# A stick-breaking layer rebuilt on sigmoids and a reversed scan, with a respaced HGRN2 layer, in a four-layer decoder trunk

## The chip, the cores and the metric

The kernel runs on one core of a Trainium2 chip as one launch. The metric is the device time of that launch in microseconds (us): 2760.55 before, the median of three runs (2756.59 to 2761.02). The core's engines each work through a queue of their own, in order: TensorE (PE: matmuls and transposes; PEld is its weight load), VectorE (DVE), ScalarE (ACT), GpSimd (POOL) and SyncE (SP, which issues the transfers). They wait for each other by semaphores.

## The reference, cut to what matters

One batch of 512 tokens with 1024 features goes through four layers, each a token mixer and a gated FFN, each with modulation before and a LayerNorm over the residual behind. The change touches the mixers of layer 1 (HGRN2, 8 heads of 128) and layer 3 (stick-breaking attention, 16 heads of 64).

```python
# HGRN2, in chunks of 32 tokens
scores = einsum(q * exp(b - b_ref), k * exp(b_ref - b))        # b: cumsum of log f in the chunk
o_intra = einsum(where(causal, scores, 0), v)
def step(S, (qd, kd, vc, dec)):
    o = einsum('bthd,bhdv->bthv', qd, S)
    S = dec[..., None] * S + einsum('bshd,bshv->bhdv', kd, vc)
...
# stick-breaking, per block of 128 queries t over all keys s before them
z = einsum('bthd,bshd->bhts', q, k)          # q already times 64 ** -0.5
neg_log_1mb = where(valid, softplus(z), 0)   # valid: s < t
later = cumsum(neg_log_1mb, axis=s, reverse=True) - neg_log_1mb
a = where(valid, exp(log_sigmoid(z) - later), 0)
o = einsum('bhts,bshd->bthd', a, v)
```

Since exp(log_sigmoid(z)) is sigmoid(z) and exp(-softplus(z)) is sigmoid(-z), a(t,s) is also sigmoid(z(t,s)) times the product of sigmoid(-z(t,s')) over s < s' < t.

## The kernel before

Activations lie feature-major in SBUF as a high and a low part (fp32r), and every projection takes three matmuls for each product (high by high, low by high, high by low). A *unit* is one 128x1024 block of weights: a transfer into a `raw` buffer (three of them), a cast to the high part on ACT (L255), a subtraction for the low part on DVE (L257), and 24 matmuls of 512 columns. `up` (L285) makes one block of 128 features from a unit; the `down` helpers (L354, L406) make token-major output and hand each piece to `evict`, which adds it to the residual X and at the end of a token block t runs the LayerNorm and the transposes (`tr`) for the next sublayer. `settle` (L480, L481) multiplies and shifts X by the LayerNorm's gain and bias, eight DVE operations that are not needed before the next residual; they take two of the `raw` buffers while they run.

**HGRN2** (`hgrn`). After the values (`p_hv`) come 24 units, q, f and gate for each head (`p_hqf`, `p_hg`). `decay(hd)` makes the decayed queries and keys of a head (QP, KP, QD, KD) on ACT and DVE. `mix(hd)` is a generator in six pieces: `hkz` transposes KD; `hS` makes the scores; `hkv` the 15 chunk products, and behind them on DVE the state chain S (L859), 15 steps, each from the one before; `ho` first the part inside a chunk (L866, *intra*), then 32-row tiles from the states (L870, *inter*, which reads S step by step); `hot` transposes the result. PE's order is written out by hand: units stand at whole numbers, the pieces of a pair's two heads at `d` plus the numbers in HA and HB (HA_END, HB_END for the last pair, whose `d` comes two units earlier), and the list is sorted. The other engines are ordered by the scheduler, by the order of emission and by `high_priority`. `settle` is called when the second pair's decays are emitted. The last pair is filled with the output projection (`down_late`): `early` gives the (half, weight pair) steps that are put among the pieces, `bridge` those that follow, and what is left goes token block by token block at the end.

**Stick-breaking** (`stick`). After the values (`p_sv`) and `settle`, each of 8 pairs of heads takes two units (`p_sqk`, L285), scores z with keys on the partitions (L1236; two fp32r matmuls each, since q and k are stored with their low parts in the other head's rows), a softplus in four passes on ACT and DVE over 1280 columns, its cumulative sum over the keys by matmuls with triangles of ones (L1265, c), exp, a mask, and the product with the values (L1284, so; fp32, two heads side by side). STEPS sets the order of emission; PE's order is the scheduler's.

Of the kernel before, what the change touches and what calls it, by code (L numbers as in the profile page):

```python
# [72 lines left out]
def pack(inp):  # L73
# [70 lines left out]
class Trunk:  # L144
# [243 lines left out]
    def down_late(self, w, nk, act, name, evict, early, bridge, gate=None, rowc=None):  # L388
# [8 lines left out]
        def load(h, kp):  # L397
            return self.unit(w, h * npair + kp, name, None if gate is None else gate[:, h * T:(h + 1) * T], rowc)
# [27 lines left out]
        hls = [[load(h, kp) for kp in left[h]] for h in range(2)]  # L426
# [290 lines left out]
    def hgrn(self, nxt):  # L717
# [4 lines left out]
        with tc.tile_pool(name="hg", bufs=1, reuse_waits="tile") as op, ExitStack() as es:  # L722
# [42 lines left out]
            self.down(ins["hv"], KD, hid, "hv", 2, put_v, head=HEAD)  # L765
            self.psum(mm="01", sc="2", kv="3456", sm="7")
# [59 lines left out]
            def mix(hd, stag, QP, KP, QD, KD_, dec):  # L826
# [30 lines left out]
                for n in range(NC - 1):  # L857
                    Sn = hp.tile([P, P], F32, tag="S", bufs=SB, name=f"S{hd}_{n}")
                    nc.vector.scalar_tensor_tensor(out=Sn, in0=Ss[n], scalar=dec[:, n:n + 1],  # L859
                                                   in1=pv[n % 4][:, n // 4 * P:(n // 4 + 1) * P], op0=ALU.mult, op1=ALU.add)  # L860
                    Ss.append(Sn)
# [65 lines left out]
            next(run[H - 1])  # L927
            self.psum(mm="345601", tr="27")
# [220 lines left out]
    def stick(self, nxt):  # L1149
# [3 lines left out]
        offs = [0, 512, 1024, 896]  # L1153
        with tc.tile_pool(name="so", bufs=1, reuse_waits="tile") as op, ExitStack() as es:
# [11 lines left out]
            stri = kp.tile([P, P], F32, name="stri")  # L1166
            nc.sync.dma_start(out=stri, in_=ins["stri"])
            smask = kp.tile([P, P], I32, name="smask")
            nc.sync.dma_start(out=smask, in_=ins["smask"])
            nu = self.sp.tile([P, T], F32, tag="u", bufs=4, name="nu")[:, 0:P]  # L1170
            nc.sync.dma_start(out=nu, in_=ins["negu"])
            negu = kp.tile([P, P], F32R, name="negu")
            nc.vector.tensor_copy(negu, nu)
            negone = kp.tile([P, P], F32R, name="negone")
            nc.vector.tensor_scalar(out=negone, in0=self.onesr.bitcast(F32), scalar1=-1.0, scalar2=None, op0=ALU.mult)
            self.psum(mm="01", z="237", c="456")
            with tc.issue_after(last[-1].ins):
                nc.scalar.preload_act_table_set("natural_log_exp_and_others")
            gate = self.gate_rows(op, i, 0, "mm")
            free = [(kp, f"n{j}") for j in range(QKS)] + [(op, f"o{j}") for j in range(2 * KD)]  # L1180

            def slot(name, keep=False):
                s = next(f for f in free if not keep or f[0] is op)
                free.remove(s)
                z = s[0].tile([P, T], F32R, tag=s[1], name=name)
                z_slot[name] = s
                return z

            def drop(name):
                s = z_slot.pop(name)  # L1190
                free.insert(sum(f[0] is kp for f in free) if s[0] is kp else len(free), s)

            z_slot = {}
            own = [slice(HD * hh, HD * hh + HD) for hh in range(2)]
            seg = ((0, 512), (512, 1024), (1024, 1280))

            def diags(z):

                return (z[:, 0:1024].rearrange("p (a c) -> p a c", a=2)[:, :, 0:P],
                        z[:, 896:1152].rearrange("p (a c) -> p a c", a=2))  # L1200

            def two(m):
                return m.rearrange("p (a c) -> p a c", a=1).broadcast_to([P, 2, P])

            def queries(p):

                qs = [slot(f"sq{p}{hh}") for hh in range(2)]
                pq = self.up(ins["sqk"], p, "sqk")
                for hh in range(2):
                    r, o = own[hh], own[1 - hh]  # L1210
                    nc.scalar.mul(qs[hh][r, :], pq[r, :], HD ** -0.5)
                    nc.vector.scalar_tensor_tensor(out=qs[hh][o, :], in0=pq[r, :], scalar=HD ** -0.5,
                                                   in1=qs[hh][r, :].bitcast(F32), op0=ALU.mult, op1=ALU.subtract)
                return qs

            def keys(p):
                ks, kx = ([slot(f"{n}{p}{hh}") for hh in range(2)] for n in ("sk", "sx"))
                pk = self.up(ins["sqk"], KD + p, "sqk")
                for hh in range(2):
                    r, o = own[hh], own[1 - hh]  # L1220
                    nc.scalar.copy(ks[hh][r, :], pk[r, :])
                    nc.vector.tensor_tensor(out=ks[hh][o, :], in0=pk[r, :], in1=ks[hh][r, :].bitcast(F32), op=ALU.subtract)
                    nc.scalar.copy(kx[hh][o, :], pk[r, :])
                    nc.vector.tensor_copy(kx[hh][r, :], ks[hh][o, :].bitcast(F32))
                return ks, kx

            def scores(p, hh, qs, ks, kx):
                zt = kp.tile([P, 1280], F32, tag="zt", bufs=ZTB, name=f"zt{p}{hh}")
                for g, (s0, s1) in enumerate(seg):
                    zb = self.bank(f"z{g}_{p}{hh}", "z")  # L1230
                    for sb in range(NT):
                        lo, hi = max(s0, offs[sb]), min(s1, offs[sb] + T - sb * P)
                        if lo < hi:
                            t0 = sb * P + lo - offs[sb]
                            for kk in (ks, kx):
# [164 lines left out]
```

## Time and profile before

| | |
|---|---|
| median of three runs | 2760.55 us |
| the profiled execution, its own time | 2756.47 us |
| its span, first to last instruction | 2754.6 us |
| HGRN2, first q unit to first FFN matmul | 671.5 to 937.6 us |
| stick-breaking, first q unit to first FFN matmul | 2141.4 to 2376.7 us |

The times of rows are microseconds from the span's start. PE's matmuls are pipelined: a matmul of 512 columns is listed with 0.39 us, but the next starts 0.23 us later, so prices are taken from start to start. A tile's name is the program's; a fp32 matmul is two records, a transpose or an fp32r matmul one.

### The profile page before, as it was taken

How to read it: one execution, taken by the hardware profiler on the slowest of the kernel's cores; microseconds unless marked ns; L12 is line 12 of the kernel's file. 1: busy time of each engine (PE TensorE's matmuls, PEld its weight loads, DVE VectorE, ACT ScalarE, POOL GpSimd, SP SyncE). 2: the span in 40 equal slices, each digit the busy share in tenths (PEclk: the TensorE clock that was granted, in tenths of full speed). 3: DMA queues.
4: the chain of work that ended last, by engine and by line, in shares of the span. 5: the costliest groups of instructions: out<-in, count | busy, mean ns of one | idle time of the engine just before them, and what ended most of it. 6: DMA issues, size and time to landing. Idle time of an engine off the chain costs nothing.

```text
span 2754.6 us, 33739 instructions
## 1 busy us (share of the span) xinstructions
PE 2655.6 (96%) x12980; PEld 2128.7 (77%) x12980; DVE 2027.7 (74%) x3133; ACT 1270.9 (46%) x1773; POOL 43.7 (2%) x80
## 2 busy tenths in 40 slices
PE   7979999999998999999999999999999999999998
PEld 5538888877776788887887777888887777888886
DVE  7558997674777699667756777997676688766676
ACT  3134433345674443334545444443334798543432
POOL 0000000000000000000000000000000000000000
PEclk9989999999999999999999999999999999999999
DMA  9844874222221386232222322873333211333222
GB/s 322 235 110 155 299 236 143 95 100 89 85 72 45 126 295 222 92 102 92 98 79 77 97 79 95 276 258 121 100 103 99 62 48 31 106 100 110 97 92 77
DMA packets 109673, 352.33 MB, mean 128 GB/s; under 512 B 12104, under 2 KB 22600, under 8 KB 109512
## 3 DMA queue, kind: packets, MB, share of 16 engines
q1 hardware_dynamic: 109512, 350.17, 38.5%
q8 instruction: 102, 1.67, 0.2%
q14 instruction: 59, 0.48, 0.1%
HBM read 341.63 MB, written 8.50 MB: 127 GB/s over the span
## 4 chain that ended last, share of the span: by engine, by line
PE 79%; DVE 9%; ACT 8%; DMA 2%; issue 2%; POOL 1%; SPq 0%; POOLq 0%; DVEq 0%; ACTq 0%
PE p_f L285 34%; PE p_d L354 16%; PE p_mup L285 5%; PE p_pw L285 3%; PE p_mdn L354 3%; PE p_hqf L285 2%; PE p_hv L354 1%; PE p_sv L354 1%; PE pc L683 1%; PE p_pw L354 1%; PE p_hg L285 1%; PE p_hwo L406 1%; PE ms L977 1%; PE tr L512 1%; ACT hf L517 1%
## 5 line engine op out<-in xcount | busy, mean ns | idle before, releaser
L285 PE MATMUL p_f<-hh,wh_f 128*128 128x512 f32 (+1 forms) x1504 | 565.4, 377 | 1.5 <-ACT hh L523 1.5
L285 PE MATMUL p_f<-hl,wh_f 128*128 128x512 f32 (+1 forms) x1504 | 566.5, 377 | 0.0
L285 PE MATMUL p_f<-hh,wl_f 128*128 128x512 f32 (+1 forms) x1504 | 565.6, 376 | 0.0
L255 ACT CAST wh_f<-r_f 128x1024 fp32r<-128x1024 f32 x176 | 185.2, 1054 | 345.1 <-PE p_f L285 310.1
L285 PEld LDWEIGHTS p_f<-hh,wh_f 128*128 128x128 f32 x1504 | 284.0, 189 | 53.1 <-ACT hh L523 1.8
L285 PEld LDWEIGHTS p_f<-hl,wh_f 128*128 128x128 f32 x1504 | 284.2, 189 | 51.1 <-issue 0.2
L285 PEld LDWEIGHTS p_f<-hh,wl_f 128*128 128x128 f32 x1504 | 284.1, 189 | 51.3 <-issue 0.2
L257 DVE TENSOR_TENSOR wl_f<-r_f,wh_f 128x1024 fp32r<-128x1024 f32 x176 | 215.1, 1224 | 133.8 <-ACT wh_f L255 133.1
L211 DVE CUSTOM_DVE_ANT_0 ada<-ada,sbc,adab 128x1024 f32<-128x1024 f32 x192 | 243.9, 1280 | 6.8 <-DMA ada<-in_ada_dram 6.8
L1331 DVE SCALAR_TENSOR_TENSOR cv<-p_f,par,cv 128x511 f32<-128x511 f32 (+1 forms) x176 | 131.4, 746 | 1.4
L1331 DVE SCALAR_TENSOR_TENSOR cg<-p_f,par,cg 128x511 f32<-128x511 f32 (+1 forms) x176 | 131.3, 746 | 1.3
L245 DVE TENSOR_TENSOR r_d<-r_d,gate 128x1024 f32<-128x1024 f32 x88 | 107.5, 1222 | 28.5 <-DMA r_d<-in_fdn_dram 27.7
L1341 ACT ACTIVATE cg<-cg 128x512 f32<-128x512 f32 x88 | 55.5, 630 | 154.9 <-DVE cg L1331 154.9
L257 DVE TENSOR_TENSOR wl_d<-r_d,wh_d 128x1024 fp32r<-128x1024 f32 x88 | 107.5, 1221 | 11.7 <-ACT wh_d L255 11.7
L285 PE MATMUL p_mup<-hh,wh_mup 128*128 128x512 f32 (+1 forms) x280 | 107.4, 384 | 0.9 <-ACT hf L517 0.9
L285 PE MATMUL p_mup<-hh,wl_mup 128*128 128x512 f32 (+1 forms) x280 | 106.3, 380 | 0.0
L285 PE MATMUL p_mup<-hl,wh_mup 128*128 128x512 f32 (+1 forms) x280 | 105.9, 378 | 0.0
L255 ACT CAST wh_d<-r_d 128x1024 fp32r<-128x1024 f32 x88 | 92.4, 1050 | 20.5 <-PE p_f L285 16.6
L626 ACT ACTIVATE X<-X,mv 128x512 f32<-128x512 f32 x56 | 43.0, 811 | 79.4 <-DVE mv L614 79.4
L1329 ACT ACTIVATE cg<-p_f,par 128x512 f32<-128x512 f32 x88 | 68.2, 774 | 13.2 <-PE p_f L285 13.2
L1329 ACT ACTIVATE cv<-p_f,par 128x512 f32<-128x512 f32 x88 | 68.1, 774 | 3.9 <-PE p_f L285 3.9
L354 PE MATMUL p_d<-wl_d,gr2h 128*128 128x512 f32 x176 | 69.6, 396 | 0.0
(510 smaller groups left out, 5868.0 us busy)
## 6 DMA issues: line engine op xcount, KB each, us to landing
ada<-in_ada_dram SPq DMA_DIRECT2D x192, 512.0 KB, 4.6
r_f<-in_fup_dram SPq DMA_DIRECT2D x176, 512.0 KB, 3.9
r_d<-in_fdn_dram SPq DMA_DIRECT2D x88, 512.0 KB, 3.3
r_mup<-in_mup_dram SPq DMA_DIRECT2D x32, 512.0 KB, 3.3
r_pw<-in_pw_dram SPq DMA_DIRECT2D x24, 512.0 KB, 7.5
r_hqf<-in_hqf_dram SPq DMA_DIRECT2D x16, 512.0 KB, 3.3
r_mdn<-in_mdn_dram SPq DMA_DIRECT2D x16, 512.0 KB, 3.3
r_sqk<-in_sqk_dram SPq DMA_DIRECT2D x16, 512.0 KB, 3.6
```

The costliest lines, as they stand in the source:

```text
L211: nc.vector.tensor_tensor_reduce(out=raw, in0=raw, in1=self.sbc, scale=1.0, scalar=ab[:, j:j + 1], op0=ALU.mult, op1=ALU.add, accum_out=ac ...
L245: nc.vector.tensor_tensor(out=r, in0=r, in1=gr, op=ALU.mult)
L255: nc.scalar.copy(hi, raw)
L257: nc.vector.tensor_tensor(out=lo, in0=raw, in1=hi.bitcast(F32), op=ALU.subtract)
L285: self.nc.tensor.matmul(ps[:, c0:c1], a, b[:, k, c0:c1], start=(n == 0), stop=(n == 3 * KD - 1))
L354: self.nc.tensor.matmul(bank, l[:, ts_], r, start=(kp == first and a == n == 0), stop=(kp == last and a == 1 and n == 2))
L406: self.nc.tensor.matmul(bank, l[:, ts_], r, start=(kp == first and a == n == 0), stop=(kp == last and a == 1 and n == 2))
L512: nc.tensor.transpose(ps[:, j * P:(j + 1) * P], n[:, k * P:(k + 1) * P], self.ident)
L626: nc.scalar.activation(out=o[:, hs], in_=x[:, hs], func=AF.Identity, scale=mv[:, 2:3], bias=mv[:, 3:4])
L1329: nc.scalar.activation(out=o, in_=ps, func=AF.Identity, scale=w[2], bias=par[:, C_CONVB + m:C_CONVB + m + 1])
L1331: nc.vector.scalar_tensor_tensor(out=o[:, s:], in0=ps[:, :T - s], scalar=w[2 - s], in1=o[:, s:], op0=ALU.mult, op1=ALU.add)
L1341: nc.scalar.activation(out=cg, in_=cg, func=AF.Silu)
```

## The change

In HGRN2 the pieces get other places (HA, HB and the two for the end), the state chains and the decay of head 6 get priority on the engines that the scheduler orders, `settle` is called right after the values, all scores of the last pair use bank `sc`, and of the output projection one more weight pair is left for the end (`early` and `bridge` change), whose last two units get buffers of their own (`spare`).

In stick-breaking q and k are stored once, in fp32; z is made with queries on the partitions, the two heads in row tiles of 64; ACT makes sigmoid(z) and sigmoid(-z) from each bank; a DVE scan that runs from the last key to the first (multiply, then maximum with a mask that sets 1 from the diagonal on) makes the products, one multiplication makes a; PE transposes a (`at`), ACT and DVE copy it out with the mask; the product with the values follows. PE's order is written out by hand, in half units, and the output projection is put in by `down_late`.

```diff
-HA = (1.5, 1.5, 2.5, 2.5, 3.5, 4.5)
-HB = (2.52, 3.52, 3.53, 4.9, 4.9, 5.9)
-HA_END = (1.5, 1.5, 2.5, 2.5, 3.5, 4.5)
-HB_END = (2.52, 3.52, 3.53, 4.9, 4.9)
+HA = (1.6, 1.7, 2.3, 2.6, 4.3, 5.8)
+HB = (2.4, 3.1, 4.32, 5.4, 6.3, 8.0)
+HA_END = (1.5, 1.55, 2.35, 3.65, 3.7, 4.7)
+HB_END = (2.4, 2.8, 3.72, 4.8, 4.9)
+SPRIO = 200
-ZTB, SPB, SHB, SLB = 4, 2, 1, 1
+BB, AB = (2, 3), (2, 2)
...
+    dg = (p_ <= f_).astype(np.float32)
+    o["sown"] = np.concatenate([dg * x for x in (0, 0, 0, 1, 1, 0, 1)], axis=1)
...
-        hls = [[load(h, kp) for kp in left[h]] for h in range(2)]
+        last = [(h, kp) for h in range(2) for kp in left[h]][-2:]
+        hls = [[load(h, kp, spare if (h, kp) in last else None) for kp in left[h]] for h in range(2)]
...
             self.down(ins["hv"], KD, hid, "hv", 2, put_v, head=HEAD)
+            self.settle()
...
+                with tc.high_priority(offset=SPRIO):
+                    for n in range(NC - 1):
...
-                    run[hd] = mix(hd, "sc" if hd % 2 else "sm", *decay(hd, *pj.pop(hd)))
-                if pr == 1:
-                    self.settle()
+                    with tc.high_priority(offset=SPRIO + 100 if act is None and hd % 2 == 0 else 0):
+                        dec = decay(hd, *pj.pop(hd))
+                    run[hd] = mix(hd, "sc" if hd % 2 or act is None else "sm", *dec)
...
-                                [(1, (0, 1, 2))], (0, 1, 2), gate=gate, rowc=ng)
+                                [(1, (0, 1)), (0, (0,))], (1, 2), gate=gate, rowc=ng,
+                                spare=lambda tag, nm: late["p"].tile([P, D], F32R, tag="tw", bufs=4, name=nm))
...
-            self.psum(mm="01", z="237", c="456")
+            self.psum(mm="01", z="234", t="56", o="7")
...
+            cols = (((3, 0),), ((2, 0), (0, 384)), ((1, 512),))
...
+            def scores(p, g):
...
+                for b, c in cols[g]:
+                    w = (b + 1) * P
+                    for hh in range(2):
+                        r = slice(HD * hh, HD * hh + HD)
+                        nc.tensor.matmul(zb[hh][:, c - c0:c - c0 + w], q[r, b * P:(b + 1) * P], k[r, 0:w], start=True, stop=True,
+                                         tile_position=(HD * hh, 0))
+                    n = c - c0 + w
+                for hh in range(2):
+                    for name, sc in (("g", -1.0), ("b", 1.0)):
+                        nc.scalar.activation(out=st[name, p, part][hh][:, c0:c0 + n], in_=zb[hh][:, 0:n], func=AF.Sigmoid,
+                                             scale=sc * HD ** -0.5)
...
+                    nc.vector.tensor_tensor_scan(out=G[:, ::-1], data0=G[:, ::-1], data1=masks[part][:, ::-1], initial=1.0,
+                                                 op0=ALU.mult, op1=ALU.max)
+                    nc.vector.tensor_tensor(out=B[:, 0:w - 1], in0=B[:, 0:w - 1], in1=G[:, 1:w], op=ALU.mult)
...
+            for p in range(KD):
+                for z, u in (("q", p), ("k", KD + p)):
+                    for half in range(2):
+                        todo.append((2 * p + (z == "k") + half / 2, lambda u=u, d=(z, p), half=half: project(u, d, half)))
+                for at, fn in ((2.4, lambda p=p: scores(p, 0)), (2.9, lambda p=p: scores(p, 1)), (3.4, lambda p=p: scores(p, 2)),
+                               (4.4, lambda p=p: turn_a(p, 0)), (4.9, lambda p=p: values(p, (3,))), (5.4, lambda p=p: turn_a(p, 1)),
+                               (5.9, lambda p=p: turn_c(p)), (6.4, lambda p=p: values(p, (2, 0, 1)))):
```

On DVE, the state chain of HGRN2's first head (S, its steps numbered) before: X is `settle`'s, G and KP a later head's decay, wl a unit's low part.

```order
L859 SCALAR_TENSOR_TENSOR S_0_5460<-S_4752,ex_5282,hkv_0_5441 128x128
L817 TENSOR_TENSOR G_5387<-B_5735 128x512
L859 SCALAR_TENSOR_TENSOR S_1_5462<-S_0_5460,ex_5282,hkv_1_5442 128x128
L481 TENSOR_TENSOR X_84<-X_84,pnb_1_5776 128x1024
L859 SCALAR_TENSOR_TENSOR S_2_5464<-S_1_5462,ex_5282,hkv_2_5443 128x128
L480 TENSOR_TENSOR X_85<-X_85,png_1_5774 128x1024
L859 SCALAR_TENSOR_TENSOR S_3_5466<-S_2_5464,ex_5282,hkv_3_5444 128x128
L821 TENSOR_TENSOR KP_5743<-K_5386,F_5385 128x512
L859 SCALAR_TENSOR_TENSOR S_4_5468<-S_3_5466,ex_5282,hkv_0_5441 128x128
L481 TENSOR_TENSOR X_85<-X_85,pnb_1_5776 128x1024
L859 SCALAR_TENSOR_TENSOR S_5_5470<-S_4_5468,ex_5282,hkv_1_5442 128x128
L257 TENSOR_TENSOR wl_hqf_5796<-r_hqf_5792,wh_hqf_5794 128x1024
```

The same head's chain on DVE in the change:

```order
L859 SCALAR_TENSOR_TENSOR S_0_5472<-S_4752,ex_5294,hkv_0_5453 128x128
L859 SCALAR_TENSOR_TENSOR S_1_5474<-S_0_5472,ex_5294,hkv_1_5454 128x128
L859 SCALAR_TENSOR_TENSOR S_2_5476<-S_1_5474,ex_5294,hkv_2_5455 128x128
L820 TENSOR_TENSOR KP_5728<-K_5398,F_5397 128x512
L859 SCALAR_TENSOR_TENSOR S_3_5478<-S_2_5476,ex_5294,hkv_3_5456 128x128
L859 SCALAR_TENSOR_TENSOR S_4_5480<-S_3_5478,ex_5294,hkv_0_5453 128x128
```

Of what stood between the steps only KP is left; the steps up to S_14 follow without a break.

On DVE, the chain of the last head (7) in the change, at the end of the layer: `r_hwo` scales an output unit's raw weights by the gate, X takes partial sums, og, hos and wl belong to the output projection.

```order
L859 SCALAR_TENSOR_TENSOR S_0_6921<-S_4752,ex_6509,hkv_0_6902 128x128
L244 SCALAR_TENSOR_TENSOR r_hwo_7133<-r_hwo_7133,hng,gate_0_5049 128x1024
L859 SCALAR_TENSOR_TENSOR S_1_6923<-S_0_6921,ex_6509,hkv_1_6903 128x128
L579 SCALAR_TENSOR_TENSOR X_82<-X_82,pe_hwo_0_6958 128x512
L859 SCALAR_TENSOR_TENSOR S_2_6925<-S_1_6923,ex_6509,hkv_2_6904 128x128
L859 SCALAR_TENSOR_TENSOR S_3_6927<-S_2_6925,ex_6509,hkv_3_6905 128x128
L579 SCALAR_TENSOR_TENSOR X_83<-X_83,pe_hwo_1_6959 128x512
L859 SCALAR_TENSOR_TENSOR S_4_6929<-S_3_6927,ex_6509,hkv_0_6902 128x128
L887 TENSOR_TENSOR og_4737<-hot_6974,SG_6163 128x512
```

Here the steps are still apart: between S_0 and S_14 stand one r_hwo, four X, two og, two hos and one wl; before, one r_hwo followed S_0 in the same way and two wl, two X, a second r_hwo, an og and a hos came in the later steps.

On PE, one pair's stretch of stick-breaking in the change: `so` is the value product of the pair before, `at` its transposes, z the scores of the pair after.

```order
L1262 MATMUL so_17224<-sa_17308,sv_16686 64x128 x2
L1262 MATMUL so_17224<-sa_17308,sv_16687 64x128 x2
L1236 MATMUL at_10_17353<-ident,sb_17194 128x128 x4
L1236 MATMUL at_11_17360<-ident,sb_17195 128x128 x4
L1205 MATMUL z_20_17371<-sk_17306,sq_17222 128x512
L1205 MATMUL z_21_17372<-sk_17306,sq_17222 128x512
L282 MATMUL p_sqk_17322<-hh_16500,wh_sqk_17318 128x512
```

Before, a head's 20 c matmuls stood in such a place, the first of them these:

```order
L1265 MATMUL c_30_17784<-sh_17718,negu 128x512
L1265 MATMUL c_30_17784<-sl_17719,negu 128x512
L1265 MATMUL c_30_17784<-sh_17718,negone 128x384
L1265 MATMUL c_30_17784<-sl_17719,negone 128x384
L1265 MATMUL c_30_17784<-sh_17718,negone 128x256
```

All 40 c matmuls of a pair are gone, 20 transposes of 128 columns come, and every piece now has half a unit (12 matmuls) behind it.

## Rows read from the trace of the kernel before

**Rows 1.** Part 1 of the page: busy time, share of the span, instructions.
```profile
PE 2655.6 (96%) x12980; PEld 2128.7 (77%) x12980; DVE 2027.7 (74%) x3133; ACT 1270.9 (46%) x1773; POOL 43.7 (2%) x80
```

**Rows 2.** Windows of HGRN2: length, then busy time of each engine, PE's clock, DMA.
```profile
671.50:715.46 43.96, 43.96 (x194) 36.15 (x193) 23.71 (x37) 30.92 (x39) 0.00 (x0) 1.00 0.28 95
715.46:768.50 53.04, 48.91 (x317) 37.98 (x316) 43.88 (x80) 34.52 (x49) 2.44 (x2) 0.94 0.23 73
768.50:815.02 46.52, 45.19 (x318) 36.38 (x317) 35.46 (x72) 34.57 (x49) 2.30 (x2) 1.00 0.24 78
815.02:862.44 47.42, 40.45 (x265) 29.16 (x264) 38.96 (x77) 31.41 (x48) 2.42 (x2) 0.93 0.14 46
862.44:907.67 45.23, 37.67 (x268) 27.49 (x266) 26.53 (x52) 11.83 (x20) 2.02 (x2) 0.92 0.15 47
907.67:937.63 29.96, 26.23 (x122) 20.75 (x120) 19.43 (x36) 13.41 (x21) 1.12 (x2) 0.98 0.30 100
```

**Rows 3.** Groups of lines, HGRN2, PE: busy us, mean ns, idle before, releaser.
```profile
L870 PE MATMUL ho<-S,QD 128*32 128x128 f32 x256 | 27.3, 300 | 17.0 <-DVE S L859 16.9
```

**Rows 4.** Timeline of PE in HGRN2: start, us, instruction.
```profile
750.57 1.08 PE L870 MATMUL ho<-S,QD 128*32 128x128 f32 x32
...
768.50 0.60 PE L831 MATMUL hkz<-ident,KD 128*128 128x128 f32 x4
768.94 1.06 PE L839 MATMUL hS<-QP,KP 128*128 128x128 f32 x8
769.75 0.47 PE L285 MATMUL p_hg<-hh,wh_hg 128*128 128x512 f32 x1
...
775.39 1.17 PE L854 MATMUL hkv<-hv,kt 32*128 32x128 f32 x30
776.49 1.16 PE L866 MATMUL ho<-hv,sT 128*128 128x128 f32 x8
```

**Rows 5.** Timeline of DVE, state chain of the first head.
```profile
728.93 0.34 DVE L859 SCALAR_TENSOR_TENSOR S<-S,ex,hkv 128x128 f32<-128x128 f32 x1
...
737.46 2.64 DVE L859 SCALAR_TENSOR_TENSOR S<-S,ex,hkv 128x128 f32<-128x128 f32 x7
```

**Rows 6.** Timeline of DVE, state chain of the last head.
```profile
883.66 0.34 DVE L859 SCALAR_TENSOR_TENSOR S<-S,ex,hkv 128x128 f32<-128x128 f32 x1
887.46 1.28 DVE L247 SCALAR_TENSOR_TENSOR r_hwo<-r_hwo,hng,gate 128x1024 f32<-128x1024 f32 x1 [3.46 <-DMA r_hwo<-in_hwo_dram]
...
898.87 0.73 DVE L859 SCALAR_TENSOR_TENSOR S<-S,ex,hkv 128x128 f32<-128x128 f32 x2
```

**Rows 7.** Window of stick-breaking's values, with `settle` in it; columns as in rows 2.
```profile
2100.39:2137.91 37.52, 37.52 (x168) 31.06 (x167) 21.94 (x30) 13.72 (x21) 0.00 (x0) 1.00 0.39 125
```

**Rows 8.** Window of one stick-breaking pair; then its PE time by line.
```profile
2256.73:2279.41 22.68, 22.09 (x122) 17.72 (x121) 20.73 (x29) 20.66 (x27) 0.00 (x0) 1.00 0.15 47
2256.73:2279.41 22.68, 11.35 (x49) 8.87 (x48) 1.00 0.15 47
2256.73:2279.41 22.68, 2.92 (x16) 2.57 (x16) 1.00 0.15 47
2256.73:2279.41 22.68, 6.41 (x40) 5.52 (x40) 1.00 0.15 47
2256.73:2279.41 22.68, 2.38 (x17) 1.06 (x17) 1.00 0.15 47
```

**Rows 9.** Groups of lines, ACT and DVE: busy us, mean ns.
```profile
L781 ACT ACTIVATE E<-p_hqf 128x512 f32<-128x512 f32 x8 | 4.8, 599 | 0.1
L1238 ACT COPY zt<-z 128x256 f32<-128x256 f32 x16 | 6.1, 382 | 0.0
L807 DVE TENSOR_TENSOR_SCAN B<-rst,F 128x512 f32<-128x512 f32 x8 | 9.8, 1222 | 0.1
L257 DVE TENSOR_TENSOR wl_hqf<-r_hqf,wh_hqf 128x1024 fp32r<-128x1024 f32 x14 | 17.1, 1221 | 13.4 <-ACT wh_hqf L255 13.4
L1276 DVE TENSOR_TENSOR zt<-zt,smask 128x256 int32<-128x256 int32 x32 | 12.1, 419 | 1.4 <-ACT zt L1273 1.3
```

More of the change, by code (lines that the diff above doesn't have):

```diff
@@ L395, in down_late, with load @@
         left[0] = [kp for kp in left[0] if kp not in bridge]
-        def load(h, kp):
-            return self.unit(w, h * npair + kp, name, None if gate is None else gate[:, h * T:(h + 1) * T], rowc)
+        def load(h, kp, into=None):
+            return self.unit(w, h * npair + kp, name, None if gate is None else gate[:, h * T:(h + 1) * T], rowc, into=into)
         def mm(bank, h, t, kp, hl, first, last):
@@ L927, in hgrn @@
             next(run[H - 1])
+            vs.close()
+            late["p"] = es.enter_context(tc.tile_pool(name="hw", bufs=1, side="right", reuse_waits="tile"))
             self.psum(mm="345601", tr="27")
@@ L1180, in stick @@
[L1180 to L1208, printed above, removed]
-                for hh in range(2):
[L1210 to L1214, printed above, removed]
@@ L1227, in scores @@
[L1227 to L1235, printed above, removed]
-                                nc.tensor.matmul(zb[:, lo - s0:hi - s0], kk[hh][:, sb * P:(sb + 1) * P],
-                                                 qs[hh][:, t0:t0 + hi - lo], start=(kk is ks), stop=(kk is kx))
-                    nc.scalar.copy(zt[:, s0:s1], zb[:, :s1 - s0])
-                for n in ("sq", "sk", "sx"):
-                    drop(f"{n}{p}{hh}")
-                return zt
@@ new lines, in stick, with project @@
+            gate = self.gate_rows(op, i, 0, "mm")
+            W = (T, 768)
+            cols = (((3, 0),), ((2, 0), (0, 384)), ((1, 512),))
+            masks = (own[:, 0:T], own[:, P:7 * P])
+            st = {}
+            def project(u, dst, half):
+                if half == 0:
+                    st["hl"] = self.unit(ins["sqk"], u, "sqk")
+                    st["pq"] = self.bank(f"p_sqk_{u}")
+                    self.up_mm(st["pq"], st["hl"], 0, T, range(4))
+                    return
+                self.up_mm(st["pq"], st["hl"], 0, T, range(4, KD))
+                z = st[dst] = kp.tile([P, T], F32, tag=dst[0], bufs=2, name=f"s{dst[0]}{dst[1]}")
+                nc.scalar.copy(z, st["pq"])
@@ new lines, in turn_a @@
+            def turn_a(p, part):
+                a = st["a", p, part] = [kp.tile([P, T], F32, tag=f"a{part}", bufs=AB[part], name=f"sa{part}{p}{hh}") for hh in range(2)]
+                for hh in range(2):
+                    ps = self.bank(f"at{part}_{p}{hh}", "t")
+                    for x in range(4):
+                        nc.tensor.transpose(ps[:, x * P:(x + 1) * P], st["b", p, part][hh][:, x * P:(x + 1) * P], self.ident)
+                    evict(ps, a[hh], 0, (384, 256)[part], (384, 256)[part])
@@ new lines, in stick @@
+            for z in range(8):
+                todo.append((2 * KD + z / 2, lambda: next(dn)))
+            todo.sort(key=lambda x: x[0])
+            with tc.manual_schedule(engines={mybir.EngineType.PE}):
+                for _, fn in todo:
+                    fn()
+                values(KD - 1, (2, 0, 1))
+            self.due = i, 0
+            es.close()
+            late["p"] = es.enter_context(tc.tile_pool(name="sf", bufs=1, reuse_waits="tile"))
+            self.psum(mm="234501", tr="67")
@@ L1317, in ffn @@
+            for _ in dn:
+                pass
     def ffn(self, i, nxt):
```

160 lines of the change are left out of this document (62 added, 98 removed).

## The prediction

> **What bounds the kernel now.** Read the page first: PE is busy in 96% of the span [rows 1], so only what shortens PE's work or its waits can show. The diff touches two layers, so the next views are theirs. In HGRN2 the windows show a layer that starts full (8 units in 43.96 us, 5.5 us each, clock 1.00) and then does not: the later windows have idle PE time and clocks of 0.92 to 0.94 [rows 2]. The clock that a row grants is a share of the upper level (2.4 GHz); 0.92 means that part of the stretch ran at the lower one (1.2 GHz), and those parts follow waits. Who is waited for stands in the groups of lines: the inter matmuls (L870) hold PE for 27.3 us busy and 17.0 us idle, all of it for the state chain S on DVE [rows 3], where a head without a wait takes 1.08 us [rows 4]. That is 44.3 us for what costs 8 x 1.08 = 8.6 us. The timeline of DVE says why: the first head's 15 steps, 0.35 us each, go from 728.93 to 740.1, because `settle`'s operations and others stand between them [rows 5]; the last head's go from 883.66 to 899.6, with 3.5 us of waiting for a transfer among them [rows 6].
>
> In stick-breaking it is PE's work that sets the pace. One pair takes 22.68 us, and PE is busy in 22.09 of them, with ACT at 20.66 and DVE at 17.72 close behind [rows 8]. By line, PE spends 11.35 us on projections, 2.92 on z, 6.41 on the cumulative sums c and 2.38 on the value product [rows 8], in the order of its rows.
>
> **The change in HGRN2.** What the layer would take without waits, from the rows: a unit 5.5 us; a head's pieces hkz 0.44, hS 0.81, hkv 1.10, intra 1.0, inter 1.08, hot as hkz 0.44 [rows 4], together 4.9, and about 0.1 at each switch. The windows of rows 2 hold, in order from the second: 6 units and two heads (43.2 against 53.04: 9.8 lost); the same (46.52: 3.3 lost); 4 units and two heads but for one hot (31.7 against 47.42: 15.7 lost); 90 output matmuls at 0.229 and two to three of each piece (31.6 against 45.23: 13.6 lost); the last 102 output matmuls and 16 transposes (25.1 against 29.96: 4.9 lost). The losses make 47.3 us, of 222.2.
>
> Moving the pieces costs nothing in PE work: the same matmuls run. It puts two units and more (13 us) between hkv and inter where one unit stood (5.6 us), against a chain of 15 x 0.35 = 5.2 us. For the first head of a pair the chain is now nearly unbroken, so its wait goes. For the second head DVE's order still has a decay's addition, scan, subtraction and product, a low part and an og among the steps, 5.6 us in all, so 10.8 us and some waiting for ACT's logarithms, against 12.4 us of cover: I leave 0.5 us a pair. What is late next there is nothing that the rows show: DVE's own work for a pair is 38 us of 43.
>
> At the end of the layer less is gained. Head 5's chain has 9.4 us of other work in it, 14.6 in all, and PE reaches its inter 11 us after hkv: 3.5 us of wait. Head 6's decay gets priority, but head 7's transpose (hkz) still stands behind that long chain: 1.3 us. Head 7's chain keeps 8 us of other work and a transfer: r_hwo_7133 takes a raw buffer that comes free about 2 us before S_0, and in the row before such a transfer was waited for 3.5 us [rows 6]. So it ends some 15.7 us after hkv, with 7.4 us of cover (24 matmuls, two hots and the intra): 7 us of wait stay. The fuller tail (18 matmuls for each token block where there were 12) covers most of the 4.9 lost in the last window; I leave 1.5. The lower clock behind the waits that are left takes 2, and 1 goes on odd switches. Sum: 1 + 3.5 + 1.3 + 7 + 1.5 + 3 = 17.3 left of 47.3, so **30 us gained**; bounds: 15 (the end does not improve and the second heads wait 2 us each) and 43 (all but 4 goes).
>
> `settle` moves to the values, eight DVE operations and two transfers that go through SP ahead of the q units' weights. The same call stands at the same place in stick-breaking, where PE was busy for all of 37.52 us while DVE had 21.94 us of work, settle included [rows 7]; so I cost it at nothing, and 2 us if the first weights come late.
>
> **The change in stick-breaking.** Per pair, on PE. Gone: z 2.92 and c 6.41. Projections stay, 11.35, cut in four instead of two: 11.5. New z: 1280 columns for each head in fp32, two heads in row tiles. Two column tiles of the value product go side by side and take 2.38 for 1280 columns [rows 8]; serial would be 4.8. For row tiles the nearest row is hkv: 15 fp32 matmuls of 128 columns in 1.10 us (775.39 to 776.49), 0.073 each, where whole-array ones of that size take 0.81 / 4 = 0.20 (hS) [rows 4]; four row tiles do overlap, 2.8 times. I take 2.4. Transposes: 20 at 0.11 (hkz, four in 0.44): 2.2. Value product: the same 1280 columns, in pieces of 128: 2.4. Sum 18.5.
>
> Then the wait that this makes. DVE's work per pair: two scans of 512 at 1.22 and two of 768 at 1.8; products of 511 and 767 columns, 0.69 and 0.95 (between 0.42 for 256 and 1.22 for 1024); two low parts, 2.44; masks on 128 and 256 columns, 1.8; the low part of the output, 0.69: 14.3 us [rows 9]. ACT: eight sigmoids of 512 at 0.60, four of 256 at 0.38, about 4 us of copies, and the two casts that it had [rows 9]: some 12.4. Neither fills 18.5. But one path is tight. From z of block 1 on, DVE has in order two scans of 768, a product, a low part, the other product and the last mask: 0.5 + 3.6 + 0.95 + 1.22 + 0.95 + 0.42 = 7.7 us before the last value matmuls may start; PE reaches them after 12 matmuls, four transposes, 12 matmuls and 8 value matmuls, 2.8 + 0.45 + 2.8 + 0.9 = 7.0. So PE waits some 0.9 us in each pair, 19.4 in all against 22.68. Eight pairs: 8 x 3.3 = 26 us. The two pieces of ACT work that went (softplus, exp) had no other reader, and the first table load moves with the first sigmoid; I take fill, output projection (192 matmuls as before) and tail as they were, but give 1 us for a tail with hand-set order. **27 us gained**; bounds 8 (z serial, 2.4 x 8 less) and 36 (no DVE wait, a shorter drain).
>
> **The sum.** Against the profiled execution: 2756.5 - 30 - 27 = 2699.5. The profiled execution is 4.1 below the median of the three runs, so for a median I say **2701**.
>
> **The rivals.** *HGRN2's chains stay broken* (0.14). The order shows head 5's and head 7's chains still mixed with other work. If the second heads and the end lose as before, 15 is gained instead of 30: 2716.
>
> *The reversed scan is dearer* (0.10). No row shows a scan with a negative step; the forward one costs 1.22 for 512 [rows 9]. At twice that, the path above takes 11.4 us against 7.0, so a pair takes 18.5 + 4.4 = 22.9 and stick-breaking gains nothing: 2728. (The Trainium skill, Vector Engine (DVE) Microarchitecture Reference, section 5.1, lists how the engine streams an operand with a negative step as not measured.)
>
> *Slower than before* (0.03). It is the same mechanism further on: DVE's load per pair is 8.3 us without scans and 2 x 1280 scanned elements at 2.3 ns. The whole kernel loses from where a pair takes 22.7 + 30 / 8 = 26.4 us, which is 7.1 ns an element, three times the forward row. At four times a pair takes 31.6 us: 8 x (31.6 - 22.7) = 71 lost, 30 gained, 2801. For it speaks only that no row excludes it.
>
> *PE waits for banks* (0.06). z has three banks, each scores call takes two, and each bank is held until two sigmoids have read it. A call's four sigmoids are 2.4 us on ACT, with a cast of 1.05 and a copy of 0.6 ahead of them at worst 4; PE is back after 12 matmuls and some pieces, 3.7. That could cost 0.3 to 1.5 us in a pair: up to 12 us, 2713. The Trainium skill says it as a rule (TensorEngine Tiling (Array Packing), PSUM Bottleneck): tiling makes the matmuls faster but not the reading of PSUM, which may become the bound. By that rule this rival would hold; the load of ACT falls from 20.66 to 12.4 by the rows, so I keep it small.
>
> *Row tiles of 64 do not overlap* (0.05): 2.4 more in a pair, 2720. Against it stand hkv's rows.
>
> *Nearly all waits go* (0.07): HGRN2 gains 43, stick-breaking 36: 2681.
>
> **How the numbers follow.** The forecast has 0.53, and no change, within 5.5 us (0.2% of the time, about what a measurement of this kernel can tell), 0.02: the two gains lie in different layers and do not depend on one another. The slow scan has the 0.03 left for slower. All else is faster: 0.95. The range reaches from the case of few waits, with 9 us below it for a shorter drain, to the dear scan with 4 us above it: 2672 to 2732; what lies outside is mostly the slow case.
>
> **What would show it.** Right: in HGRN2 the idle time before L870 falls from 17.0 us to some 5, nearly all of it in the last three heads, and the three loop windows take 43 to 44 us per 6 units; the c groups are gone, a pair takes 19 to 19.5 us, with a wait of PE for DVE's last mask before the value product; row tiles start within some 10 ns of each other; a scan of 768 takes 1.8 us. Wrong: a scan of 3 us or more; z matmuls of the two heads one after the other; PE idle before z for ACT's sigmoids; p_hqf late behind `settle`; or a longer tail behind the output projections.

## The result and the profile after

| | before | after |
|---|---|---|
| median | 2760.2 us (4 runs, 2756.6 to 2761.0) | 2718.07 us (4 runs, 2717.6 to 2719.9) |
| ratio, 95% interval | | 0.9851 (0.9834 to 0.9868) |
| profiled execution, its span | 2756.47, 2754.6 us | 2719.89, 2718.1 us |

The change is 42 us faster where 59 were forecast; the range (2672 to 2732) holds the time. Page part 1 of after, to set beside [rows 1]:

```profile
PE 2620.6 (96%) x13012; PEld 2099.0 (77%) x13012; DVE 1991.0 (73%) x3051; ACT 1192.1 (44%) x1750; POOL 43.3 (2%) x80
```

PE is still busy in 96% of the span. The stages, each from its first matmul to that of the next one, read from the two timelines, say which layer gave what:

| stage, us | before | after |
|---|---|---|
| all up to HGRN2's first unit | 671.5 | 674.0 |
| HGRN2 | 266.1 | 255.0 |
| its FFN | 371.8 | 370.2 |
| layer 2's mixer (not in the diff) | 412.2 | 413.8 |
| its FFN | 370.6 | 370.6 |
| stick-breaking's values and `settle` | 49.1 | 47.8 |
| stick-breaking, pairs and tail | 235.4 | 208.3 |
| the rest | 377.9 | 378.4 |

Stick-breaking gave 28.5 us with its values (27 forecast), HGRN2 11.1 (30 forecast). The stages that no edit touches differ by up to 2.5 us, and more between other kernels below; so the experiments are judged by the stage they touch and by the total only beside it.

HGRN2 after, windows with the columns of [rows 2] (length; busy time of PE, PEld, DVE, ACT and POOL, with instructions; granted clock; DMA share and GB/s):

```profile
674.01:717.98 43.97, 43.97 (x194) 36.16 (x193) 23.71 (x37) 30.91 (x39) 0.00 (x0) 1.00 0.29 95
717.98:765.50 47.52, 44.84 (x328) 37.08 (x327) 35.45 (x72) 37.19 (x52) 2.07 (x2) 1.00 0.20 68
765.50:811.00 45.50, 42.12 (x307) 34.41 (x305) 35.35 (x73) 32.39 (x46) 2.03 (x2) 1.00 0.21 70
811.00:836.39 25.39, 25.12 (x197) 21.02 (x197) 20.73 (x40) 19.80 (x27) 0.00 (x0) 0.93 0.19 63
836.39:866.77 30.38, 18.71 (x96) 14.26 (x93) 20.83 (x40) 13.27 (x21) 2.05 (x1) 0.66 0.11 35
866.77:898.31 31.54, 28.82 (x231) 21.69 (x228) 25.59 (x53) 8.33 (x16) 2.02 (x2) 0.95 0.15 51
898.31:928.99 30.68, 29.21 (x134) 22.93 (x133) 21.27 (x40) 15.00 (x27) 2.12 (x3) 1.00 0.24 74
```

The first loop window, the second row, has the full clock now (1.00 where [rows 2] had 0.94), but one stretch of 30 us holds only 18.7 us of PE work at a granted clock of 0.66. The groups of lines of PE in this layer (busy us, mean ns, idle before, releaser) say what is waited for:

```profile
L870 PE MATMUL ho<-S,QD 128*32 128x128 f32 x256 | 11.6, 285 | 0.8 <-DVE S L859 0.8
L838 PE MATMUL hS<-QP,KP 128*128 128x128 f32 x64 | 10.4, 314 | 4.5 <-ACT ob L882 3.7 <-ACT kt L832 0.7
L866 PE MATMUL ho<-hv,sT 128*128 128x128 f32 x64 | 9.5, 296 | 8.7 <-ACT ob L882 8.7
...
L830 PE MATMUL hkz<-ident,KD 128*128 128x128 f32 x32 | 5.5, 298 | 0.9 <-DVE og L887 0.9
```

Against [rows 3], the inter matmuls went from 27.3 + 17.0 us to 11.6 + 0.8: 31.9 us gained on the very wait that the change is about, somewhat more than the whole forecast for the layer. But 20.8 of it came back as other time. L866 and hS, which waited for nothing before (idle 0.0 in the same view), now wait 8.7 and 4.5 us, nearly all of it for `ob`, the scaled output of the head before. The two groups before:

```profile
L839 PE MATMUL hS<-QP,KP 128*128 128x128 f32 x64 | 9.5, 295 | 0.0
L866 PE MATMUL ho<-hv,sT 128*128 128x128 f32 x64 | 8.9, 281 | 0.0
```

Follow `ob` for head 4, whose inter matmuls end at 835.3. The timeline, PE, ACT, DVE and POOL:

```profile
850.90 2.08 PE L866 MATMUL ho<-hv,sT 128*128 128x128 f32 x8 [8.74 <-ACT ob L882]
```
```profile
840.89 0.60 ACT L797 ACTIVATE SG<-p_hg 128x512 f32<-128x512 f32 x1
841.38 0.59 ACT L873 ACTIVATE sTsq<-ho 128x512 f32<-128x512 f32 x1
...
849.70 1.14 ACT L882 ACTIVATE ob<-ho,ms 128x128 f32<-128x128 f32 x4 [4.09 <-POOL ms L879]
```
```profile
846.18 0.34 DVE L859 SCALAR_TENSOR_TENSOR S<-S,ex,hkv 128x128 f32<-128x128 f32 x1
846.44 0.68 DVE L875 TENSOR_REDUCE ms<-sTsq 128x4 f32<-128x512 f32 x1
847.04 0.34 DVE L859 SCALAR_TENSOR_TENSOR S<-S,ex,hkv 128x128 f32<-128x128 f32 x1
847.29 0.16 DVE L877 TENSOR_SCALAR ms<-ms 128x4 f32<-128x4 f32 x1
```
```profile
847.62 2.05 POOL L879 TENSOR_TENSOR ms<-ms,mhalf 128x4 f32<-128x4 f32 x1 [37.58 <-DVE ms L877]
```

The square (L873) comes 6.0 us after the matmuls, behind other ACT work, in which two table loads (ACT_TABLE_LOAD, at 836.10 and 839.59) take 1.28 us each; its sum (L875) 4.5 us later, in the midst of head 5's chain; then scale, power on POOL, and `ob`, which ends at 850.84. The five operations' own work is 4.6 us and their path 15.5; what covers it on PE is little more than one unit (5.6). All heads' `ho` share one bank, `sm`, with the even heads' hS of the first three pairs, and it comes free only with `ob`: so intra of head 5 starts at 850.90.

Stick-breaking, one pair, beside the first of [rows 8]; and DVE's groups of scans and masks:

```profile
2198.13:2217.32 19.19, 19.19 (x126) 14.39 (x125) 13.51 (x16) 10.92 (x22) 0.00 (x0) 1.00 0.19 57
```
```profile
L1218 DVE TENSOR_TENSOR_SCAN sg<-sg,sown 128x768 f32<-128x768 f32 x16 | 27.2, 1743 | 3.0 <-ACT sg L1210 3.0
L1218 DVE TENSOR_TENSOR_SCAN sg<-sg,sown 128x512 f32<-128x512 f32 x16 | 19.2, 1216 | 5.8 <-ACT sg L1210 5.8
L1227 DVE TENSOR_TENSOR sa<-at,smask 128x256 int32<-128x256 int32 x24 | 9.7, 420 | 9.5 <-ACT sa L1224 9.5
```

A pair takes 19.19 us (19.4 forecast), all of it PE work. The scan with a negative step takes 1216 ns for 512 columns, as the forward one of [rows 9] (1222).

### The profile page after: what moved, and what is told of

Read it like the earlier page. It is cut to its first block, busy times and chain, and to the rows that moved or that the text cites. A ratio compares the mean times of both kernels' runs of the same rounds, so it can differ in the third digit from the quotient of the medians.

```text
span 2718.1 us, 33772 instructions
## 1 busy us (share of the span) xinstructions
PE 2620.6 (96%) x13012; PEld 2099.0 (77%) x13012; DVE 1991.0 (73%) x3051; ACT 1192.1 (44%) x1750; POOL 43.3 (2%) x80
## 4 chain that ended last, share of the span: by engine, by line
PE 81%; DVE 8%; ACT 5%; DMA 3%; issue 2%; POOL 1%; SPq 0%; POOLq 0%; DVEq 0%; ACTq 0%
PE p_f L282 35%; PE p_d L351 16%; PE p_mup L282 6%; PE p_mdn L351 3%; PE p_hqf L282 2%; PE p_sqk L282 2%; PE p_pw L282 2%; PE p_hv L351 1%; PE p_sv L351 1%; PE p_pw L351 1%; DMA ada<-in_ada_dram 1%; PE ms L981 1%; ACT hf L515 1%; PE p_hg L282 1%; DMA r_swo<-in_swo_dram 1%
## 5 line engine op out<-in xcount | busy, mean ns | idle before, releaser
L242 DVE TENSOR_TENSOR r_d<-r_d,gate 128x1024 f32<-128x1024 f32 x88 | 107.5, 1222 | 27.7 <-DMA r_d<-in_fdn_dram 26.7
L351 PE MATMUL p_d<-wl_d,gr0h 128*128 128x512 f32 x176 | 69.6, 396 | 0.0
```

Source lines behind the costliest of these rows:

```text
L242: nc.vector.tensor_tensor(out=r, in0=r, in1=gr, op=ALU.mult)
L351: self.nc.tensor.matmul(bank, l[:, ts_], r, start=(kp == first and a == n == 0), stop=(kp == last and a == 1 and n == 2))
```

## The experiments

The theory: HGRN2's missing 19 us are the path to `ob`, queued on ACT and DVE without priority, and the clock that PE loses behind the long wait. The rival: DVE and ACT have no room in the last pair, whatever goes first. HGRN2's stage in each run:

| kernel | HGRN2, us | idle before L870, L866, hS, hkz | median, us |
|---|---|---|---|
| before | 266.1 | 17.0, 0, 0, 0 | 2760.2 |
| stick_only | 264.8 | 16.2, 0, 0, 0 | 2731.1 |
| the change | 255.0 | 0.8, 8.7, 4.5, 0.9 | 2718.1 |
| old_places | 259.6 | 9.1, 0, 2.9, 0 | 2721.8 |
| settle_back | 257.5 | 2.5, 8.6, 3.3, 0 | 2724.7 |
| no_chain_prio | 249.2 | 1.6, 4.4, 5.6, 0.9 | 2713.1 |
| rms_first | 246.6 | 1.4, 1.5, 8.0, 0.9 | 2710.4 |
| rms_no_chain_prio | 246.7 | 1.6, 3.0, 5.6, 0.9 | 2709.9 |
| rms_hs_later | 253.9 | 1.9, 1.3, 3.6, 8.9 | 2718.7 |
| rms_hs_kt | 254.4 | 1.9, 1.4, 4.1, 9.0 | 2715.2 |
| all_scores_sc | 256.1 | 1.8, 2.8, 12.0, 0.4 | 2718.8 |
| z_one_row_tile | 253.1 | 0.5, 8.8, 4.4, 0.9 | 2729.0 |

Two of these kernels have the HGRN2 lines of another: stick_only those of before (264.8 us against 266.1), z_one_row_tile those of the change (253.1 against 255.0). So the stage moves by up to 1.9 us with nothing changed in it, and a difference of about that size shows nothing.

**stick_only**: every HGRN2 line as before.

```diff
-HA = (1.6, 1.7, 2.3, 2.6, 4.3, 5.8)
...
-SPRIO = 200
+HA = (1.5, 1.5, 2.5, 2.5, 3.5, 4.5)
...
+SPRIO = 0
...
+                if pr == 1:
+                    self.settle()
```

> Stick-breaking of the change with HGRN2 of before (times, no priority, settle with the second pair, tail and bridge of before). If the two layers add up: HGRN2 266 us as before, stick-breaking 210 us as in the change, total 2760.2 - 28.6 = 2731.6, within 2729 to 2734. If part of the HGRN2 edit's gain is paid elsewhere, or the stick-breaking gain rests on it, the total is under 2727 or over 2737.

2731.08 us, ratio 0.9898 (0.9884 to 0.9913); stick-breaking's pairs and tail take 208.5 us, as in the change (208.3). The two layers add up: 29 us for stick-breaking alone, where its stages gave 28.5; the 13 that are left of the 42 stand against 11.1 in HGRN2's stage.

**rms_first**: priority for the path to `ob`.

```diff
+                with tc.high_priority(offset=100):
+                    sq = wt("sT", f"sq{hd}")
+                    nc.scalar.activation(out=sq, in_=po, func=AF.Square)
...
+                        nc.scalar.mul(ob[:, b * P:(b + 1) * P], po[:, b * P:(b + 1) * P], ms[:, 4 + b:5 + b])
```

> The change, with priority (offset 100) also for the five operations that follow a head's inter matmuls: square, sum, scale, power, ob. Theory A: HGRN2 gained 11 us and not 30 because the wait of PE went from the state chain to the end of this path: bank sm comes free only with ob, and in the changed kernel PE waits for ob 8.7 us before intra of head 5 and 1.8 to 1.9 us before hS of heads 4 and... of the two later pairs. Then the wait before intra falls under 2 us, those before hS under 0.7, the clock windows 811:858 and 858:903 rise from 0.83 and 0.87 to over 0.93, HGRN2 takes 238 to 246 us instead of 255.0, and the total is 2702 to 2710. Rival B: DVE and ACT have no room there, and what is put ahead delays the chain or a decay as much; the wait shows before L870, hkz or hot instead, HGRN2 takes 252 to 258, the total is 2715 to 2721.

2710.4 us, ratio 0.9824 (0.9808 to 0.984); HGRN2 246.6 us, 8.4 less. PE's groups in this run:

```profile
L870 PE MATMUL ho<-S,QD 128*32 128x128 f32 x256 | 11.9, 288 | 1.4 <-DVE S L859 1.4
L838 PE MATMUL hS<-QP,KP 128*128 128x128 f32 x64 | 9.0, 285 | 8.0 <-ACT kt L832 4.3 <-ACT ob L882 3.7
L866 PE MATMUL ho<-hv,sT 128*128 128x128 f32 x64 | 8.6, 276 | 1.5 <-ACT ob L882 1.5
```

The wait before L866 falls from 8.7 to 1.5 and the chains do not suffer (L870 1.4): the theory's main term is shown. The clock follows: between 811 and 903 us the granted clock is 0.94, where the change has 0.85. Stage and total end just outside theory A's ranges, and two things did not go as expected. The waits before hS in the loop stay (3.7 in both kernels); the square before head 2's hS still starts 4.9 us after the matmuls (760.05 in the change, 756.42 here), behind ACT work that this priority does not pass. And 3.7 us of a new one appear, head 6's hS waiting for `kt`, which stands on ACT behind a cast and an exponential that waits for DVE. So part of the rival holds too: some of the gain only moved one piece on.

**no_chain_prio**: no priority for the state chains.

```diff
-                with tc.high_priority(offset=SPRIO):
+                if True:
                     for n in range(NC - 1):
```

> The change without priority for the state chains (that of head 6's decay stays). Theory A: the steps stand among other work again, the chains end later, and PE waits for S before L870 (3 to 10 us instead of 0.8), while ob comes about as late; HGRN2 256 to 264 us, total 2719 to 2727. Rival C: it is the chain's priority that holds back the sum of squares of the head before; without it ob comes earlier and HGRN2 takes 246 to 253, total 2709 to 2716.

HGRN2 249.2 us, median 2713.06, ratio 0.9831 (0.9812 to 0.9851): rival C held, and the change is faster without this part of itself. DVE in this run, where the sum of squares stood in the midst of the chain in the change:

```profile
839.75 1.22 DVE L806 TENSOR_TENSOR_SCAN B<-rst,F 128x512 f32<-128x512 f32 x1
840.88 0.66 DVE L875 TENSOR_REDUCE ms<-sTsq 128x4 f32<-128x512 f32 x1
...
843.34 0.34 DVE L859 SCALAR_TENSOR_TENSOR S<-S,ex,hkv 128x128 f32<-128x128 f32 x1
```

The sum now comes ahead of head 5's first step, the wait before L866 is 4.4 us, and the chains, given their wider places, still end in time (L870 1.6).

**rms_no_chain_prio**: both edits.

> The change with priority for the path to ob and without priority for the chains, all places as in the change. By the run without chain priority HGRN2 took 249.2 us, by the run with priority for the path to ob 246.6, against 255.0. If the two are the same wait (the chain's priority is what held the sum of squares back), the second one adds nothing: HGRN2 245 to 248 us, total 2708 to 2712. If they are two different costs, they add: HGRN2 239 to 243 us, total 2702 to 2707. If the chains are the next bound once they lose their place, L870 waits over 4 us and HGRN2 takes 249 us or more.

HGRN2 246.7 us, 2709.91, ratio 0.9818 (0.9801 to 0.9834). The first case held, the two gains are one: once the path to `ob` has priority, the chains' own priority neither helps nor hurts. This and rms_first are the fastest kernels of the study.

**old_places**: HA, HB, HA_END and HB_END of before, all else as in the change.

> The change with the step places HA, HB, HA_END, HB_END of before; priorities, settle, banks and tail stay those of the change. Theory A: the respacing is what removed the waits for the state chain, since a unit (5.6 us) alone doesn't cover a chain of 15 steps at 0.35 us plus what stands between: L870 waits 6 to 14 us again, HGRN2 258 to 268 us, total 2721 to 2732. Rival: the chain's priority alone removes them; L870 waits under 4 us and HGRN2 takes 248 to 257 us, total 2710 to 2720.

HGRN2 259.6 us, median 2721.8. Theory A held: L870 waits 9.1 us again, and L866 not at all. The wider places take nearly all of the chain's wait, for with them and without the chains' priority it is 1.6 us (no_chain_prio). With the narrow places it falls from 17.0 to 9.1; how much of that is the priority and how much `settle`'s new place, no run tells apart. Why the trace of before shows no wait for `ob` can be read on ACT; before, head 4:

```profile
836.16 0.60 ACT L873 ACTIVATE sTsq<-ho 128x512 f32<-128x512 f32 x1 [2.46 <-PE ho L870]
...
839.17 1.14 ACT L882 ACTIVATE ob<-ho,ms 128x128 f32<-128x128 f32 x4 [0.87 <-POOL ms L879]
```

While PE waited for S, ACT ran out of work and waited for the inter matmuls itself, 2.5 us (1.7 in old_places). So the path to `ob` took 4.2 us (6.5 in old_places) and not 15.5. For hS the new places count too: from the end of head 1's inter matmuls PE came to head 2's hS after 17.3 us before, and after 7.1 in the change.

**settle_back**:

```diff
-            self.settle()
             self.psum(mm="01", sc="2", kv="3456", sm="7")
...
+                if pr == 1:
+                    self.settle()
```

> The change with settle back at the second pair's decays. The prediction priced its new place at nothing to 2 us and gave its old place a part in the broken first chain. Theory A: with priority for the chains, settle delays only what has no priority (decay and sums of squares); eight operations of 1.2 us make the first two pairs wait 1 to 5 us more, total 2719 to 2723. Rival: its place was most of the gain, HGRN2 263 us or more, total over 2725.

HGRN2 257.5 us, 2.5 more than the change, of which 1.7 are waits before L870. That is little more than the 1.9 by which the stage moves unchanged: a small gain from `settle`'s new place is likely and not shown. The median, 2724.7, lies between the two ranges. The profiled spans differ by 4.3 (2722.4 against 2718.1), and layer 2's mixer, which no edit touches, takes 2.9 more.

**rms_hs_later**, **rms_hs_kt**: rms_no_chain_prio with hS and intra of a pair's first head one unit later; the second one with priority for `kt` as well.

```diff
-HA = (1.6, 1.7, 2.3, 2.6, 4.3, 5.8)
+HA = (1.6, 2.05, 2.3, 3.05, 4.3, 5.8)
```

> No priority for the chains, priority (offset 100) for square, sum, scale, power and ob, and HA = (1.6, 2.05, 2.3, 3.05, 4.3, 5.8): scores hS of a pair's first head come one unit later and intra after the next unit, so that one unit more lies between ob and the next use of bank sm. Theory A: the two waits of 1.8 and 1.9 us before hS and the one of 0.9 before hkz go, the wait before intra of head 5 stays under 2 us; HGRN2 240 to 245 us, total 2703 to 2708. Rival: hS and intra only hand the wait on (to intra for the mask, or to inter), HGRN2 246 us or more, total 2709 to 2713.

> The same with priority (offset 100) for the copy kt on ACT too. In the run with priority for the path to ob, PE waited 3.7 us before hS of head 6 for kt, which stood on ACT behind an exponential that waited for DVE. Theory A: that wait falls under 1.5 us and the clock stays higher there; HGRN2 236 to 242 us, total 2699 to 2705. Rival: the wait passes to the next operand in that place (sT, og, the gate SG), total as without it, 2703 to 2709.

HGRN2 253.9 and 254.4 us, 7 worse than rms_no_chain_prio. hS no longer waits for `ob`, but:

```profile
L830 PE MATMUL hkz<-ident,KD 128*128 128x128 f32 x32 | 5.9, 316 | 8.9 <-DVE og L887 8.9
```

This is the second head's hkz. It needs bank `sc`, which the product og empties, and og stands on DVE behind the next decay's addition and scan and a unit's low part. Both theories fell. The rivals were right that the wait is handed on, but not where (neither named hkz) nor how far: the totals, 2718.7 and 2715.2, lie above their ranges. Priority for `kt` changed nothing that shows (hS waits 3.6 and 4.1 us for it): in both runs it stands on ACT behind the same exponential and a cast.

**all_scores_sc**: rms_no_chain_prio with all scores in bank `sc`, and priority for og, SG and stick-breaking's last mask.

```diff
-                    run[hd] = mix(hd, "sc" if hd % 2 or act is None else "sm", *dec)
+                    run[hd] = mix(hd, "sc", *dec)
```

> The same, with the scores of all heads in bank sc, so that no scores call waits for ob any more, priority (offset 100) for the products og and SG, and in stick-breaking for the last mask of each pair. Theory: the waits of 1.8 and 1.9 us before hS fall to the copy kt's, about 0.7 (as in the last pair of the change), 2.3 us less in HGRN2 and 0.5 to 1 us of clock; stick-breaking loses its waits before the value product, 2.1 us. Total 3 to 6 us under the run without these. Rival: bank sc, now read by kt, mask and og in turn, hands the wait to hkz and hot (the run with later scores lost 3.4 and 5.5 us there), HGRN2 as without it or over it, total no better.

HGRN2 256.1 us: hS waits 12.0 us for `kt`, which empties the same bank. The rival held in that the wait is handed on, though to hS itself and not to hkz (0.4) or hot. In stick-breaking the waits for the last mask fall by 1 us, and its pairs and tail take 208.6 us, no less than in the change.

**z_one_row_tile**: the second head's scores are left out; the first head's are made twice, from the same 64 rows.

```diff
-                        r = slice(HD * hh, HD * hh + HD)
+                        r = slice(0, HD)
...
-                                         tile_position=(HD * hh, 0))
+                                         tile_position=(0, 0))
```

> The change with both heads' z made from the rows of the first head (the second head's scores are left out and the first head's stand twice), so both matmuls use the same 64 rows of the array. If two row tiles overlap: z without overlap costs 10 x 128 columns x 2 heads at 0.20 us for 128 columns (hS) = 4.0 us in a pair where the change has 2.76, 1.0 to 1.6 us in each of 8 pairs, total 2726 to 2731. If they didn't overlap in the change, a pair keeps its 19.2 us and the total is 2717 to 2720.

2729.0 us, ratio 0.9893 (0.9873 to 0.9913); stick-breaking 220.9 us against 208.3. The first z of a pair, of the change and then of this run:

```profile
2199.15 1.13 PE L1205 MATMUL z<-sk,sq 64*128 64x512 f32 x4
```
```profile
2201.05 1.98 PE L1205 MATMUL z<-sk,sq 64*128 64x512 f32 x4
```

In the change two heads' 512 columns take 1.06 us from start to start of the next work, here 1.91. Over a pair it is 2.76 against 4.90, more than I expected: the row tiles overlap nearly in full. Eight such pairs make 17 us, and the stage is 12.6 longer: the waits of the change for the last mask (2.1 us) are gone here, and those for partial sums in the tail fall by 1.8.

## Why the prediction was right, and where it was not

*Stick-breaking: right, but for one wait.* Per pair on PE, from start to start: projections 11.6 (11.5 forecast), z 2.76 (2.4), transposes 2.33 (2.2), value product 2.49 (2.4), together 19.2 where I had 18.5. The scan costs what the forward one does, so both rivals on its price fall, and so do the serial row tiles (z_one_row_tile is what that would have been) and the wait for z's banks (no idle time before L1205 in the page's view of lines). The Trainium skill (TensorEngine Tiling (Array Packing), PSUM Bottleneck) says that tiling speeds up TensorE and not the reading of PSUM, which may become the bottleneck. It did not here: ACT was busy for 10.9 of 19.2 us. One column was misread: the 17.72 us that the prediction gives DVE in the pair before are PEld's, and DVE had 20.73 [rows 8]; the sum does not use it. Wrong was the steady wait of 0.9 us for DVE's last mask: the first pairs have none, and only three late ones, where DVE also prepares the output's weights, wait 0.5 to 0.9 us, 2.1 in all. DVE's path, from the first scan of block 1 to the last mask, in the pair above:

```profile
2210.22 3.41 DVE L1218 TENSOR_TENSOR_SCAN sg<-sg,sown 128x768 f32<-128x768 f32 x2 [0.21 <-ACT sg L1210]
2213.54 0.93 DVE L1220 TENSOR_TENSOR sb<-sb,sg 128x767 f32<-128x767 f32 x1
2214.39 1.22 DVE L254 TENSOR_TENSOR wl_sqk<-r_sqk,wh_sqk 128x1024 fp32r<-128x1024 f32 x1
2215.53 0.95 DVE L1220 TENSOR_TENSOR sb<-sb,sg 128x767 f32<-128x767 f32 x1
2216.39 0.42 DVE L1227 TENSOR_TENSOR sa<-at,smask 128x256 int32<-128x256 int32 x1
```

It is the order that I had, but z ends at 2209.70 and the mask at 2216.81: 7.1 us, not 7.7, since from start to start each operation takes up to 0.1 us less than its listed length. PE comes to the last four value matmuls after 7.1 us too (7.0 forecast). A sum of listed lengths made a wait out of a tie. That the pair comes out at 19.19 against 19.4 is in part luck: this error (0.9 too much) and the one on PE's work (0.7 too little) cancel.

*HGRN2: direction right, size wrong, by two errors of opposite sign.* The first: I left 3.5 and 7 us of wait for the chains of heads 5 and 7 and 0.5 us a pair. L870's idle time is 0.8 us in the change and stays at 1.4 when PE no longer comes late because of `ob` (rms_first): the chains keep up. The second, and larger: "What is late next there is nothing that the rows show" is the step that failed. I counted DVE's load (38 us of 43) and did not follow who else needs the bank that inter fills. By the windows PE is idle for 22.2 us of the layer where it was for 23.7; without L870 that is 21.4 us against 6.7. Of the 14.7 more, 12.4 are waits for `ob` before L866 and hS. So the sign that six units would take 43 to 44 us did not come either: the hS of heads 0, 2 and 4 start 45.6 and 47.3 us apart.

The lower clock is the third: I gave 2 us for it, and 20.8 - 14.7 = 6 us more of PE's busy time are spent on the same work. In the stretch with 0.66 granted, a matmul of 512 columns starts 0.43 us after the one before, where the full clock has 0.23. Before it, PE stood still for 8.7 us. But that price is not fixed: in z_one_row_tile, with the same HGRN2 lines and a wait of 8.8 us in the same place, PE's busy time in the layer is 229.4 us against 232.8, at a granted clock of 0.97 against 0.95. What the runs explain of the missing 19 us has a limit as well: the best of them give 8.4 back, and none gets the 3.7 us before hS in the loop without a longer wait elsewhere.

*`settle`: right.* Priced at nothing to 2 us where it went: from the first value matmul to the first q unit it is 47.9 us before and after. What the old place would cost with the chains' priority is about what the stage moves unchanged (settle_back).

*The end of the layer: right in its last waits.* Those around its last transposes and first FFN matmuls, 3.7 us in all before (2.1 and 1.5), are 0.5 now; the fuller tail covers the LayerNorm. Two waits before output matmuls are new and were not forecast: 1.5 us for a gate product (SG) at 862.5 and 1.9 for a partial sum (X) at 886.5.

*The sum.* The profiled execution less 57 is 2699.5, and with the 4.1 added for a median it would be 2703.6; the prediction says 2701 and gives no reason for the rest. The range held the time because it reached up to the dear scan (2728 and 4 more); the forecast itself was 17 us too low.

*The rival "HGRN2's chains stay broken"* gave 2716, close to the measured 2718, by luck: the gain was missing, but not at the chains. What the runs leave open is why the same instructions of layer 2's mixer took 319.7 to 324.1 us (first `p_mup` to first `p_mdn`) from kernel to kernel; that is as much as some of the edits.

## What to carry to other kernels

When a long wait goes, list for every buffer that the waiting instruction fills or frees who needs it next, and how long its path takes with its queueing: a wait that shows nowhere before may be hidden by the very one that is removed, or come with the new places. Priority for one chain is a delay for the work it passes; give it to the path whose end PE waits for, and try it with and without, since wider places alone may do. A long wait of PE costs more than its length: some of the work behind it runs at the lower clock, though how much differs from profile to profile. Before a small difference counts, see how far a stage moves between kernels that do not differ in it.

## What was not expected of the hardware

A scan on DVE whose operands all run backwards (negative step) takes what the forward one takes: 1216 ns for 512 columns, where the forward one has 1222 [rows 9]. For 768 columns it takes 1743, and the rows have no forward one of that size. Two fp32 matmuls on row tiles of 64 rows overlap nearly in full: 1.06 us for two of 512 columns, 1.91 when both use the same rows, so full overlap would be 0.96. In the first the two start 6 ns apart.
